# The second MLP product of a decoder step: loads of the squares in GpSimd's queue, other group sizes, kept weights in the last group, and the last norms on VectorE

## The chip, the cores and the metric

The kernel runs as one program on one core of a Trainium2 chip. The metric is the device time of that program in microseconds. Three runs of the kernel before gave 2498.2, 2504.89 and 2498.74 us; their median is 2498.74 us.

## What is computed

One layer of a hybrid decoder for 1024 prompt tokens and 8 x 8 sample tokens (NT = 1088 columns), all in float32. Four token mixers feed a gated output projection; an MLP and a last norm follow. The changed part is the MLP's second product and the last norm:

```python
h2 = rmsnorm(x, p["norm_mlp_g"][l]) * (1.0 + sc2) + sh2
x = x + g2 * (jnp.square(jax.nn.relu(h2 @ p["w_mlp1"][l])) @ p["w_mlp2"][l])
...
y = rmsnorm(x, p["norm_final_g"])        # x * rsqrt(mean(x * x) + 1e-6) * g, over 1024 features
```

`w_mlp1` is 1024 x 4096 and `w_mlp2` 4096 x 1024. In the sample columns the factor g2 differs from sequence to sequence, in the prompt columns it is one number per feature.

## The kernel before, in words

Features lie on partitions in blocks of 128 and tokens in columns. Each float32 operand is split into two parts: `hi`, which ScalarE writes by a copy to the fast matmul type (line 98), and `lo`, the rest, which VectorE gets by a subtraction (line 101). A product is three matmuls, hi by hi, lo by hi and hi by lo (lines 201 to 203). `weights` (lines 151 to 161) loads a weight block of up to 4 x 128 x 128 on SyncE's queue into a tile `wst` (3 buffers) and splits it into `whi` and `wlo` (4 buffers each).

The first MLP product stores its squares in DRAM, as `asc[0]` (hi) and `asc[1]` (lo), 32 blocks k of 128 x 1088 each, by DMAs that GpSimd issues (line 1372). The second product (from line 1389) has 8 output blocks `mt` and 32 blocks k. The k are taken in groups. For each group the kernel loads the group's `ah` and `al` tiles (9 buffers each, 544 KB a tile, line 1422), and for each `mt` it multiplies them with that group's weights in four quarters of 272 columns (two tiles of PSUM with two quarters each, of four such tiles in all) and adds the result, scaled by g2, into the running sum `R[mt]` (`add_resid`). A matmul has 272 columns; one k in one quarter of one `mt` is three of them. The groups are (0,1), (2 to 7), (8 to 15), (16 to 23), (24 to 27) and (28 to 31). The first reads tiles that were kept on the chip (`KK`). A group whose k lie in two weight blocks takes two `wst` for each `mt`, the part with the lower k first. In group 1 the residual `xr` is loaded again and added to each `R[mt]` (lines 1441 to 1444).

The last group is walked in three column ranges: quarters (0,1), quarter 2, quarter 3. Each range goes over all 8 `mt`, with its weights loaded and split anew, and adds the squares of the finished `R[mt]` into `accs` (ScalarE squares into `sqt`, VectorE adds). Behind each range stands its norm (lines 1448 to 1462): a float32 matmul with ones sums `accs` over the partitions (`rms`), ScalarE makes `rstd` by a logarithm and an exponential, and the 8 blocks are scaled and stored as `y`. In the ranges (0,1) and 2, ScalarE multiplies by the gain and GpSimd by `rstd`; in the last range VectorE does both for 6 of 8 blocks.

A scheduler that simulates the program decides the order of each engine's instructions; code under `high_priority` (weights and evacuations, offset 3000) moves ahead of the rest. On the chip each engine runs its list strictly in that order, and an instruction that waits holds all behind it. The DMAs of one engine stand in its list too.

Of the kernel before, what the change touches and what calls it, by code (L numbers as in the profile page):

```python
# [9 lines left out]
F32 = mybir.dt.float32  # L10
# [4 lines left out]
OP = mybir.AluOpType  # L15
# [16 lines left out]
GN_EPS = 64e-5  # L32
LN_EPS = 1e-5
# [57 lines left out]
class Net:  # L91
# [59 lines left out]
    def weights(self, ap, prio=True):  # L151

        with self.tc.high_priority(offset=PRIO) if prio else nullcontext():
            st = self.wp.tile([128, 4, 128], F32, name="wst", tag="wst", bufs=WST)
            hi = self.wp.tile([128, 4, 128], F32R, name="whi", tag="whi", bufs=WHI)
            lo = self.wp.tile([128, 4, 128], F32R, name="wlo", tag="wlo", bufs=WHI)
# [29 lines left out]
    def gemm_quarters(self, parts, X, evac, groups):  # L186
# [4 lines left out]
        for j, (ap, ks) in enumerate(parts):  # L191
            hi, lo = self.weights(ap)
# [894 lines left out]
PRIO = 3000  # L1087
WST, WHI = 3, 4
# [7 lines left out]
def trunk_kernel(ctx: ExitStack, tc: tile.TileContext, A):  # L1096
# [252 lines left out]
    with tc.tile_pool(name="pq", bufs=4, space=PSUM, reuse_waits="tile") as net.pq:  # L1349
# [41 lines left out]
        with ExitStack() as m:  # L1391
# [4 lines left out]
            GROUPS = ((0, 1), (2, 3, 4, 5, 6, 7), tuple(range(8, 16)), tuple(range(16, 24)), (24, 25, 26, 27), (28, 29, 30, 31))  # L1396
# [16 lines left out]
            for gi, ks in enumerate(GROUPS):  # L1413
                final = gi == len(GROUPS) - 1
                Xs = {}
                for k in ks:
                    if gi == 0:
                        Xs[k] = Kept(2 * k), Kept(4 + 2 * k)
                    else:
                        t = [ap_.tile([128, NT], F32R, name=f"a{p}", tag=f"a{p}", bufs=NA) for p in "hl"]  # L1420
                        for x, d in zip(t, asc):
                            nc.sync.dma_start(x.bitcast(F32), d[k].bitcast(F32))
# [14 lines left out]
                for cs in (((0, 1),), ((2,),), ((3,),)) if final else (((0, 1), (2, 3)),):  # L1437
                    for mt in range(8):
                        net.gemm_quarters(parts(ks, mt), Y, ev, cs)
# [5 lines left out]
                    if not final:  # L1445
                        continue

                    ps = net.pqt("rms")
                    for i, q in enumerate(cs[0]):
                        sl = slice(q * QU, q * QU + QU)  # L1450
                        net.mm(ps[:, i, :QU], net.ones, accs[:, sl])
                        net.lnp(rstd[:, sl], ps[:, i, :QU], 1.0 / D, net.eps)
                        net.exph(rstd[:, sl])
                    sl = slice(cs[0][0] * QU, cs[0][-1] * QU + QU)
                    for k in range(KB8):
                        r, t = R[k][:, sl], rstd[:, sl]
                        if cs[0] != (3,) or k % 3 == 2:
                            net.act(r, r, AF.Copy, scale=net.p("norm_final_g", k))
                            nc.gpsimd.tensor_tensor(r, r, t, op=OP.mult)
                        else:  # L1460
                            net.stt(r, r, net.p("norm_final_g", k), t, OP.mult, OP.mult)
                        (nc.sync if k % 2 else nc.scalar).dma_start(A["y"][k][:, sl], r)
# [93 lines left out]
```

## Time and profile before

| | |
|---|---|
| median of three runs | 2498.74 us |
| the profiled execution | 2501.3 us, its span 2499.5 us |
| TensorE matmul | 2419.5 us busy, 97% of the span |
| VectorE, ScalarE, GpSimd | 1383.3 us (55%), 1037.4 us (42%), 331.7 us (13%) |
| mean granted TensorE clock | 0.986 of full speed |
| last column range (0,1) ends | 2449.6 us |

The span runs from the first to the last instruction; the profiled execution is 1.8 us longer than its span. All times below are microseconds from the span's start. "PE" is TensorE's matmul, "PEld" its weight load, which overlaps it, DVE is VectorE, ACT ScalarE, POOL GpSimd, and SPq is SyncE's list of DMA issues. A row that ends in [1.21 <-ACT whi] says that the engine stood idle for 1.21 us before it and which instruction ended that. The clock is given as a share of full speed: 1.00 is 2.4 GHz and 0.50 is 1.2 GHz.

### The profile page before, as it was taken

The numbers are of one execution on the slowest core, as the hardware profiler recorded it, in microseconds if no ns is written. First come the engines' busy times: TensorE is split into PE (matmuls) and PEld (weight loads), VectorE is DVE, ScalarE is ACT, GpSimd is POOL, SyncE is SP. The second block draws the span as 40 slices with busy tenths as digits, with TensorE's granted clock in tenths as the row PEclk, the third lists the DMA queues.
The fourth block names the chain that finished last, engine by engine and source line by source line (L and its number), as shares of the span: only waits on it lengthen the run. The fifth ranks groups of instructions, "written<-read, shape, count | busy, mean of one in ns | idle before, by whom it ended". The sixth has DMA issues, their size and how long they took to land.

```text
span 2499.5 us, 46627 instructions
## 1 busy us (share of the span) xinstructions
PE 2419.5 (97%) x19086; PEld 2248.1 (90%) x19086; DVE 1383.3 (55%) x2536; ACT 1037.4 (42%) x1855; POOL 331.7 (13%) x503
## 2 busy tenths in 40 slices
PE   6999999999999999999999999997999999999996
PEld 2898898998988988889888899997999999999996
DVE  6665626647265573556643767768655552422247
ACT  4513544333354224542346553455666664111115
POOL 3111210103100021010111000000222221000003
PEclk9999999999999999999999999998999999999998
DMA  6323221232321233212322464532655558435244
GB/s 245 121 89 90 67 101 63 78 99 71 105 66 62 83 94 101 73 63 84 97 85 103 143 217 154 177 124 90 174 156 153 154 148 265 148 124 186 63 157 135
DMA packets 185302, 300.46 MB, mean 120 GB/s; under 512 B 57576, under 2 KB 97464, under 8 KB 185088
## 3 DMA queue, kind: packets, MB, share of 16 engines
q1 hardware_dynamic: 134672, 217.79, 27.4%
q0 software_dynamic: 47104, 74.44, 9.8%
q10 hardware_dynamic: 3312, 5.25, 0.6%
q8 instruction: 150, 2.46, 0.4%
q14 instruction: 64, 0.52, 0.1%
HBM read 211.29 MB, written 81.66 MB: 117 GB/s over the span
## 4 chain that ended last, share of the span: by engine, by line
PE 85%; DVE 6%; DMA 3%; ACT 2%; issue 2%; SPq 0%; DVEq 0%; ACTq 0%; POOL 0%; POOLq 0%
PE pg L107 58%; PE pa L107 6%; PE pe L107 4%; PE sm L107 3%; PE pc L107 2%; PE pb L107 2%; PE ada L107 2%; PE pu L107 2%; PE G L107 1%; PE pyr L107 1%; PE po L107 1%; DVE X L101 1%; DMA adaw<-ada 1%; DMA wst<-w 1%; DVE wlo L101 1%
## 5 line engine op out<-in xcount | busy, mean ns | idle before, releaser
L107 PE MATMUL pg<-Hh,whi 128*128 128x362 f32 (+1 forms) x1872 | 627.9, 336 | 6.2 <-ACT Hh L98 4.2
L107 PE MATMUL pg<-Hh,wlo 128*128 128x362 f32 (+1 forms) x1872 | 629.4, 336 | 0.0
L107 PE MATMUL pg<-Hl,whi 128*128 128x362 f32 (+1 forms) x1872 | 620.9, 334 | 0.7 <-DVE Hl L104 0.6
L98 ACT ACTIVATE whi<-wst 128x512 fp32r<-128x512 f32 (+1 forms) x404 | 249.9, 620 | 625.7 <-PE pg L107 546.2
L101 DVE TENSOR_TENSOR wlo<-wst,whi 128x512 fp32r<-128x512 f32 (+1 forms) x404 | 279.9, 694 | 360.4 <-ACT whi L98 359.3
L107 PEld LDWEIGHTS pg<-Hh,whi 128*128 128x128 f32 x1872 | 354.2, 189 | 19.4 <-ACT Hh L98 6.0
L107 PEld LDWEIGHTS pg<-Hh,wlo 128*128 128x128 f32 x1872 | 354.6, 189 | 11.9 <-issue 4.2
L107 PEld LDWEIGHTS pg<-Hl,whi 128*128 128x128 f32 x1872 | 353.5, 189 | 10.1 <-issue 2.5
L107 PE MATMUL pg<-ah,whi 128*128 128x272 f32 x960 | 277.1, 291 | 3.7 <-ACT whi L98 3.7
L107 PE MATMUL pg<-ah,wlo 128*128 128x272 f32 x960 | 278.0, 291 | 1.1 <-DVE wlo L101 1.1
L107 PE MATMUL pg<-al,whi 128*128 128x272 f32 x960 | 274.4, 290 | 0.0
L107 PEld LDWEIGHTS pg<-ah,whi 128*128 128x128 f32 x960 | 182.5, 191 | 4.3 <-ACT whi L98 4.2
L107 PEld LDWEIGHTS pg<-ah,wlo 128*128 128x128 f32 x960 | 182.6, 190 | 1.9 <-DVE wlo L101 1.8
L107 PEld LDWEIGHTS pg<-al,whi 128*128 128x128 f32 x960 | 181.0, 190 | 0.0
L104 DVE SCALAR_TENSOR_TENSOR cacc<-u,pv,cacc 128x1024 f32<-128x1024 f32 x120 | 153.7, 1281 | 2.1
L104 DVE SCALAR_TENSOR_TENSOR R<-pg,mod,R 128x544 f32<-128x544 f32 (+2 forms) x120 | 65.7, 570 | 138.0 <-PE pg L107 138.0
L107 PE MATMUL pg<-yh,whi 128*128 128x362 f32 (+1 forms) x384 | 128.3, 334 | 1.2 <-DVE gt L101 1.1
L107 PE MATMUL pg<-yh,wlo 128*128 128x362 f32 (+1 forms) x384 | 127.2, 331 | 0.0
L107 PE MATMUL pg<-yl,whi 128*128 128x362 f32 (+1 forms) x384 | 126.8, 330 | 0.0
L1181 POOL DMA_DIRECT2D g<-gst x96 | 53.5, 557 | 385.2 <-ACT gst L98 370.3
L98 ACT ACTIVATE gst<-pg 128x362 f32<-128x362 f32 (+1 forms) x96 | 45.5, 473 | 130.5 <-PE pg L107 118.9
L693 POOL TENSOR_SCALAR sp<-St,dec 128x64 f32<-128x64 f32 x60 | 56.5, 942 | 222.8 <-DVE St L104 201.3
(446 smaller groups left out, 4818.3 us busy)
## 6 DMA issues: line engine op xcount, KB each, us to landing
wst<-w SPq DMA_DIRECT2D x136, 256.0 KB, 2.9
wst<-w_in SPq DMA_DIRECT2D x92, 256.0 KB, 2.8
gt<-g SPq DMA_DIRECT2D x32, 544.0 KB, 3.8
wst<-w_gate SPq DMA_DIRECT2D x64, 256.0 KB, 3.1
adaw<-ada SPq DMA_DIRECT2D x32, 512.0 KB, 5.3
ah<-ah POOLq DMA_DIRECT2D x60, 272.0 KB, 2.6
al<-al POOLq DMA_DIRECT2D x60, 272.0 KB, 4.3
ah<-ah SPq DMA_DIRECT2D x30, 544.0 KB, 9.6
```

Source lines behind the costliest of these rows:

```text
L98: return self.nc.scalar.activation(out, in_, func, bias=bias, scale=scale)
L101: return self.nc.vector.tensor_tensor(out, a, b, op=op)
L104: return self.nc.vector.scalar_tensor_tensor(out, a, s, b, op0=op0, op1=op1)
L107: return self.nc.tensor.matmul(out, lhsT, rhs, start=start, stop=stop, skip_group_check=True)
L693: nc.gpsimd.tensor_scalar(sp, St, dec[:, c:c + 1], None, op0=OP.mult)
L1181: nc.gpsimd.dma_start(d[:, n0:n0 + n], t[:, :n])
```

## The change

The loads of `ah` and `al` move from SyncE's list to GpSimd's. The groups become (0,1), (2,3), (4 to 11), (12 to 19), (20 to 27) and (28 to 31). `weights` can take another pool: the last group splits its 8 weight blocks once, into 8 buffers each that lie in memory that `KK` had, and all three column ranges use them. The norm of a range is written behind the third `mt` of the next range, and it is done by VectorE alone; only in the last range 2 of 8 blocks still go by ScalarE and GpSimd, as before. Two constants move to the head of the file.

```diff
-    def weights(self, ap, prio=True):
+    def weights(self, ap, prio=True, pool=None, bufs=WHI):
...
-            hi = self.wp.tile([128, 4, 128], F32R, name="whi", tag="whi", bufs=WHI)
-            lo = self.wp.tile([128, 4, 128], F32R, name="wlo", tag="wlo", bufs=WHI)
+            hi = (pool or self.wp).tile([128, 4, 128], F32R, name="whi", tag="whi", bufs=bufs)
+            lo = (pool or self.wp).tile([128, 4, 128], F32R, name="wlo", tag="wlo", bufs=bufs)
...
-        for j, (ap, ks) in enumerate(parts):
-            hi, lo = self.weights(ap)
+        for j, (W, ks) in enumerate(parts):
+            hi, lo = W if isinstance(W, tuple) else self.weights(W)
...
-            GROUPS = ((0, 1), (2, 3, 4, 5, 6, 7), tuple(range(8, 16)), tuple(range(16, 24)), (24, 25, 26, 27), (28, 29, 30, 31))
+            GROUPS = ((0, 1), (2, 3)) + tuple(tuple(range(i, i + 8)) for i in (4, 12, 20)) + ((28, 29, 30, 31),)
...
-                            nc.sync.dma_start(x.bitcast(F32), d[k].bitcast(F32))
+                            nc.gpsimd.dma_start(x.bitcast(F32), d[k].bitcast(F32))
...
-                for cs in (((0, 1),), ((2,),), ((3,),)) if final else (((0, 1), (2, 3)),):
+                def last_norm(qs):
+                    sl = slice(qs[0] * QU, qs[-1] * QU + QU)
+                    ps = net.pqt("rms")
+                    for i, q in enumerate(qs):
+                        s = slice(q * QU, q * QU + QU)
+                        net.mm(ps[:, i, :QU], net.ones, accs[:, s])
+                        net.lnp(rstd[:, s], ps[:, i, :QU], 1.0 / D, net.eps)
+                        net.exph(rstd[:, s])
+                    for k in range(KB8):
+                        r, t = R[k][:, sl], rstd[:, sl]
+                        if qs == (3,) and k % 3 == 2:
+                            net.act(r, r, AF.Copy, scale=net.p("norm_final_g", k))
+                            nc.gpsimd.tensor_tensor(r, r, t, op=OP.mult)
+                        else:
+                            net.stt(r, r, net.p("norm_final_g", k), t, OP.mult, OP.mult)
+                        (nc.sync if k % 2 else nc.scalar).dma_start(A["y"][k][:, sl], r)
+
+                columns = ((0, 1), (2,), (3,)) if final else (((0, 1), (2, 3)),)
+                if final:
+                    last.close()
+                    fw, kept = right(m, "fw"), []
+                for n, qs in enumerate(columns):
                     for mt in range(8):
-                        net.gemm_quarters(parts(ks, mt), Y, ev, cs)
+                        if not final:
+                            net.gemm_quarters(parts(ks, mt), Y, ev, qs)
+                        else:
+                            if n == 0:
+                                kept.append(net.weights(A["w2"][ks[0] // 4, mt], pool=fw, bufs=8))
+                            net.gemm_quarters([(kept[mt], ks)], Y, ev, (qs,))
...
-                    ps = net.pqt("rms")
...
-                        if cs[0] != (3,) or k % 3 == 2:
...
+                        if final and n and mt == 2:
+                            last_norm(columns[n - 1])
+                if final:
+                    last_norm(columns[-1])
```

SyncE's list where the second product begins, before; `wst` are weights (256 columns: two k, 512: four k), `xr` the residual:

```order
L159 DMA wst<-w 128x256
L1422 DMA ah<-ah 128x1088
L1422 DMA al<-al 128x1088
L1443 DMA xr<-xsp 128x544 x2
L1422 DMA ah<-ah 128x1088
L159 DMA wst<-w 128x512
L1422 DMA al<-al 128x1088
L1422 DMA ah<-ah 128x1088
```

The same place now, from the weights of group 0 on:

```order
L161 DMA wst<-w 128x256 x8
L1469 DMA xr<-xsp 128x544 x2
L161 DMA wst<-w 128x256 x7
L1469 DMA xr<-xsp 128x544 x2
L161 DMA wst<-w 128x256
L161 DMA wst<-w 128x512 x2
L1469 DMA xr<-xsp 128x544 x2
L161 DMA wst<-w 128x512 x3
```

The loads of `ah` and `al` have left the list; the weights of group 1 now stand right behind the first `xr`, and each later `xr` stands between weights.

VectorE's list in group 1, before: the evacuation of one `mt` (R_21773 is the second), the split of later weights, and the residual:

```order
L104 SCALAR_TENSOR_TENSOR R_21773<-pg,mod,R_21773 128x544
L104 SCALAR_TENSOR_TENSOR R_21773<-pg,mod,R_21773 128x272
L104 SCALAR_TENSOR_TENSOR R_21773<-pg,mod,R_21773 128x208
L101 TENSOR_TENSOR t_22279<-pg,mod 128x64
L101 TENSOR_TENSOR wlo<-wst,whi 128x512
L101 TENSOR_TENSOR R_21773<-R_21773,t_22279 128x64
L101 TENSOR_TENSOR R_21773<-R_21773,xr 128x1088
L101 TENSOR_TENSOR wlo<-wst,whi 128x256
```

Now, at the sixth `mt` of group 1 (R_21777); the first `wlo` belongs to the seventh `mt`, the second to the eighth:

```order
L106 SCALAR_TENSOR_TENSOR R_21777<-pg,mod,R_21777 128x544
L106 SCALAR_TENSOR_TENSOR R_21777<-pg,mod,R_21777 128x272
L106 SCALAR_TENSOR_TENSOR R_21777<-pg,mod,R_21777 128x208
L103 TENSOR_TENSOR t_22323<-pg,mod 128x64
L103 TENSOR_TENSOR R_21777<-R_21777,t_22323 128x64
L103 TENSOR_TENSOR wlo<-wst,whi 128x256
L103 TENSOR_TENSOR R_21773<-R_21773,xr 128x1088
L106 SCALAR_TENSOR_TENSOR R_21778<-pg,mod,R_21778 128x544
L103 TENSOR_TENSOR wlo<-wst,whi 128x256
```

The seventh block's `wlo` now stands behind the whole evacuation of the sixth, and R_21773's residual is added only there.

VectorE's list in the last group, before: the end of the range of quarter 2:

```order
L101 TENSOR_TENSOR wlo<-wst,whi 128x512
L104 SCALAR_TENSOR_TENSOR R_21776<-pg,mod,R_21776 128x272
L101 TENSOR_TENSOR accs<-accs,sqt 128x272
L101 TENSOR_TENSOR wlo<-wst,whi 128x512
L104 SCALAR_TENSOR_TENSOR R_21777<-pg,mod,R_21777 128x272
L101 TENSOR_TENSOR accs<-accs,sqt 128x272
L101 TENSOR_TENSOR wlo<-wst,whi 128x512
L104 SCALAR_TENSOR_TENSOR R_21778<-pg,mod,R_21778 128x272
```

Now, the same range (R_21777 with 272 columns from PSUM is its sixth `mt`):

```order
L103 TENSOR_TENSOR accs<-accs,sqt 128x272
L106 SCALAR_TENSOR_TENSOR R_21772<-R_21772,pv,rstd_21781 128x544
L106 SCALAR_TENSOR_TENSOR R_21773<-R_21773,pv,rstd_21781 128x544
L106 SCALAR_TENSOR_TENSOR R_21777<-pg,mod,R_21777 128x272
L106 SCALAR_TENSOR_TENSOR R_21774<-R_21774,pv,rstd_21781 128x544
L106 SCALAR_TENSOR_TENSOR R_21775<-R_21775,pv,rstd_21781 128x544
L106 SCALAR_TENSOR_TENSOR R_21776<-R_21776,pv,rstd_21781 128x544
L106 SCALAR_TENSOR_TENSOR R_21777<-R_21777,pv,rstd_21781 128x544
L106 SCALAR_TENSOR_TENSOR R_21778<-R_21778,pv,rstd_21781 128x544
L106 SCALAR_TENSOR_TENSOR R_21779<-R_21779,pv,rstd_21781 128x544
L106 SCALAR_TENSOR_TENSOR R_21778<-pg,mod,R_21778 128x272
L103 TENSOR_TENSOR accs<-accs,sqt 128x272
```

No `wlo` is left there; eight scalings of 544 columns by `rstd` stand among the evacuations, six of them in a row ahead of that of the seventh `mt`.

## Rows read from the trace of the kernel before

**Rows 1.** The first part of the page: busy us of each engine, share of the span, instructions.

```profile
PE 2419.5 (97%) x19086; PEld 2248.1 (90%) x19086; DVE 1383.3 (55%) x2536; ACT 1037.4 (42%) x1855; POOL 331.7 (13%) x503
```

**Rows 2.** The view of stretches: us, then each engine's busy us (and instructions), the granted clock, the DMA engines' mean share and GB/s.

```profile
2100.00:2150.00 50.00, 45.11 (x331) 44.07 (x330) 17.85 (x37) 8.41 (x17) 0.00 (x0) 0.93 0.58 202
2250.00:2300.00 50.00, 50.00 (x401) 50.00 (x400) 11.05 (x24) 5.06 (x8) 0.00 (x0) 1.00 0.59 220
```

**Rows 3.** TensorE's timeline, the rows with idle time ahead of them from 2103 us on: start, duration, instruction, count, and in brackets the idle time and what ended it.

```profile
2104.49 0.52 PE L107 MATMUL pg<-ah,whi 128*128 128x272 f32 x2 [1.21 <-ACT whi L98]
2110.51 0.82 PE L107 MATMUL pg<-ah,whi 128*128 128x272 f32 x2 [2.54 <-ACT whi L98]
2121.15 0.39 PE L107 MATMUL pg<-ah,wlo 128*128 128x272 f32 x1 [1.15 <-DVE wlo L101]
2451.99 0.70 PE L107 MATMUL rms<-accs,ones 128*128 128x272 f32 x2 [2.41 <-DVE accs L101]
2473.52 1.28 PE L107 MATMUL rms<-accs,ones 128*128 128x272 f32 x2 [8.22 <-DVE accs L101]
2490.97 0.70 PE L107 MATMUL rms<-accs,ones 128*128 128x272 f32 x2 [2.52 <-DVE accs L101]
```

**Rows 4.** The chain that ended last, in order of time (start, us, what): three of its pieces.

```profile
2121.15 328.44 PE pg L107 x2614
2449.61 0.80 DVE R L104
...
2494.70 1.65 DVE R L104 x4
```

**Rows 5.** The view of stretches in steps of 5 us, columns as in rows 2.

```profile
2105.00:2110.00 5.00, 2.97 (x23) 2.75 (x22) 0.00 (x0) 0.17 (x1) 0.00 (x0) 1.00 1.04 420
2110.00:2115.00 5.00, 4.49 (x18) 4.26 (x19) 0.69 (x1) 0.46 (x1) 0.00 (x0) 0.50 1.02 405
2115.00:2120.00 5.00, 5.00 (x34) 4.78 (x32) 0.99 (x2) 1.47 (x3) 0.00 (x0) 0.82 0.29 101
...
2450.00:2455.00 5.00, 3.01 (x22) 2.96 (x23) 2.31 (x5) 3.32 (x7) 0.00 (x0) 1.00 0.22 59
...
2470.00:2475.00 5.00, 1.48 (x4) 1.25 (x5) 3.47 (x7) 2.58 (x6) 0.86 (x1) 0.50 0.76 226
```

**Rows 6.** SyncE's list on the timeline, weights (line 159), and below them GpSimd's first store after 2070 us.

```profile
2059.92 21.00 SPq L159 DMA_DIRECT2D wst<-w  x6
2088.61 0.33 SPq L159 DMA_DIRECT2D wst<-w  x1
2100.26 0.33 SPq L159 DMA_DIRECT2D wst<-w  x1
2081.49 0.67 POOL L1372 DMA_DIRECT2D ah<-ah  x1 [12.01 <-ACT ah L98]
```

**Rows 7.** The DMA view: issues, KB each, median us to landing. The first two rows are of 2084 to 2103 us, the last of 1990 to 2075 us.

```profile
al<-al POOLq DMA_DIRECT2D x3, 272.0 KB, 12.3
wst<-w SPq DMA_DIRECT2D x1, 128.0 KB, 14.1
wst<-w SPq DMA_DIRECT2D x7, 128.0 KB, 2.6
```

**Rows 8.** GpSimd's DMA issues in the whole span (count, busy us, mean ns of one), and the landing times of its 16 stores of mixer outputs, 544 KB each.

```profile
L1372 POOL DMA_DIRECT2D al<-al x68 | 49.7, 814 | 44.4 <-DVE al L101 37.3 <-DVE R L101 4.2 <-DVE wlo L101 2.8
L1084 POOL DMA_DIRECT2D y<-lig x4 | 2.2, 542 | 4.0 <-DVE St L104 3.2 <-DVE lig L101 0.7
DMA to landing us min/median/max: 2.9/4.1/8.5
```

**Rows 9.** The first load for group 3 in SyncE's list, and the landing times of the 21 loads of `ah` from 2160 to 2400 us.

```profile
2273.43 0.33 SPq L1422 DMA_DIRECT2D ah<-ah  x1
DMA to landing us min/median/max: 8.5/9.5/10.6
```

**Rows 10.** The last evacuation of group 0 on ScalarE (it waits for the end of the matmuls), and the split on VectorE that ends TensorE's wait at 2121.15.

```profile
2103.32 0.81 ACT L98 ACTIVATE R<-pg,mod 128x272 f32<-128x272 f32 x2 [0.78 <-PE pg L107]
2120.68 0.41 DVE L101 TENSOR_TENSOR wlo<-wst,whi 128x256 fp32r<-128x256 f32 x1
```

**Rows 11.** VectorE's groups by shape, mean ns of one and idle time ahead: the first three from 2410 us on, the last three from 2150 to 2410 us.

```profile
L101 DVE TENSOR_TENSOR wlo<-wst,whi 128x512 fp32r<-128x512 f32 x23 | 20.7, 901 | 0.7 <-ACT whi L98 0.7
L101 DVE TENSOR_TENSOR accs<-accs,sqt 128x272 f32<-128x272 f32 x14 | 9.7, 691 | 0.6 <-ACT sqt L98 0.5
L101 DVE TENSOR_TENSOR accs<-accs,sqt 128x544 f32<-128x544 f32 x7 | 5.1, 726 | 0.9
L101 DVE TENSOR_TENSOR wlo<-wst,whi 128x512 fp32r<-128x512 f32 x43 | 29.5, 686 | 83.7 <-ACT whi L98 83.7
L104 DVE SCALAR_TENSOR_TENSOR R<-pg,mod,R 128x544 f32<-128x544 f32 x25 | 19.6, 784 | 44.0 <-PE pg L107 44.0
L101 DVE TENSOR_TENSOR R<-R,xr 128x1088 f32<-128x1088 f32 x5 | 6.5, 1292 | 0.3 <-DMA xr<-xsp 0.2
```

**Rows 12.** GpSimd's timeline in the last group: the multiplications by `rstd` of the range (0,1).

```profile
2457.97 12.88 POOL L1459 TENSOR_TENSOR R<-R,rstd 128x544 f32<-128x544 f32 x8 [363.25 <-ACT rstd L98]
```

**Rows 13.** ScalarE's timeline at the end: the logarithm behind the last `rms`, and the exponential.

```profile
2491.70 0.49 ACT L98 ACTIVATE rstd<-rms,epst 128x272 f32<-128x272 f32 x1 [1.35 <-PE rms L107]
2492.22 0.43 ACT L98 ACTIVATE rstd<-rstd 128x272 f32<-128x272 f32 x1
```

More of the change, by code (lines that the diff above doesn't have):

```diff
@@ L32 @@
 GN_EPS = 64e-5
+PRIO = 3000
+WST, WHI = 3, 4
 LN_EPS = 1e-5
@@ L1084, in lru_block @@
         nc.gpsimd.dma_start(self.ysc[3][j], hs[:, :NT])
-PRIO = 3000
-WST, WHI = 3, 4
 NG = 5
@@ L1444, in trunk_kernel @@
                             net.tt(R[mt], R[mt], x, OP.add)
-                    if not final:
-                        continue
-                    ps = net.pqt("rms")
[L1449 to L1456, printed above, removed]
-                        if cs[0] != (3,) or k % 3 == 2:
[L1458 to L1462, printed above, removed]
-    last.close()
+                        if final and n and mt == 2:
+                            last_norm(columns[n - 1])
+                if final:
+                    last_norm(columns[-1])
 def _pack(i):
```

## The prediction

> **What bounds the kernel now.** TensorE is busy for 97% of the span [rows 1], so first its pace, then its gaps. In the chain that ended last, one piece of 2614 matmuls in 328.44 us [rows 4] gives 0.12565 us a matmul; across group changes it has no gap (50.00 of 50.00 us busy and clock 1.00 [rows 2]). So the product can gain only at its two ends.
>
> At the beginning TensorE ends group 0 at 2103.28 (its next row starts at 2104.49 after 1.21 us idle [rows 3]; ScalarE's evacuation starts at 2103.32 [rows 10]). It waits 1.21, 2.54 and 1.15 us, and after the second wait the clock is 0.50 for 5 us and 0.82 for the next 5 [rows 3, 5]. From 2103.28 to 2121.15 it does 74 matmuls (2688 from the start of group 1 to the end of the range (0,1), less the 2614). At pace they take 9.3 us, so 8.6 of the 17.87 us are lost. The cause stands in SyncE's list: a block of weights is issued only at 2100.26, behind thirteen loads of squares [rows 6], while the DMA engines are full (share 1.04, 420 GB/s [rows 5]).
>
> At the end the range (0,1) is over at 2449.6 [rows 4] and the last `rms` starts at 2490.97 [rows 3]: 41.4 us for 192 matmuls (24.1 us) and three `rms` of 0.70 us (2.1). About 15 us are lost: TensorE waits 2.41, 8.22 and 2.52 us for `accs` [rows 3], and with the second wait the clock is at 0.50 again [rows 5]. VectorE is late because GpSimd multiplies beside it, 8 times 1.6 us [rows 12]: a split of weights takes 901 ns there against 686 in the middle, and an addition of 272 columns nearly as long as one of 544 (691 to 726) [rows 11].
>
> **The change, part by part.** The sum is made against the profiled execution (span 2499.5 us, 1.8 us around it). That execution is 2.6 us above the median of the runs, so the difference is taken off the median.
>
> *Loads and groups at the beginning.* The weights of group 1 stand right behind group 0's. Split number 9 (its first `mt`) can be issued when group 0's sixth block is split, about 2087 (before, it stood behind ten loads and went at 2088.61 [rows 6]). Group 1 needs it at 2103.3. Landing is between 2.6 us and 14.1 us (the same 128 KB in an idle stretch, and behind the squares [rows 7]); even the upper end gives 2101, 2102 with its split, and the next blocks come every 3 us, as their need does. So the waits of 1.21 and 2.54 us go, and the slow clock with them. The squares cannot start earlier: GpSimd's first load stands behind its store of 2081.49 [rows 6], as SyncE's did behind its weights until 2080.92. The four tiles for group 1 have 20 us; even the 14.1 us would do. The other fourteen early tiles, 7.6 MB at some 400 GB/s, are in by about 2110; group 2 begins at 2128. If the cover by distance failed, the cost is the old 8.6 us.
>
> *A new wait in group 1.* The seventh block's `wlo` stands on VectorE behind the whole evacuation of the sixth, and that needs TensorE's last matmul of the sixth. This is the wait of 1.15 us at 2121.15 once more (there too the split follows the evacuation), with one addition of 64 columns more. It waits for no DMA, only for its place. I take 1.2 us; bounds 0.9 (pipelined closer) and 1.6. Behind it stand the residual of the second block and the last two evacuations; TensorE has two PSUM tiles free then, so nothing else is late. All other `wlo` of group 1 stand ahead of their need.
>
> So the range (0,1) ends at 2103.28 + 2688 x 0.12565 + 1.2 = 2442.2 instead of 2449.6: minus 7.4 us.
>
> *Loads from GpSimd in the middle.* 60 loads of 544 KB move to GpSimd's list. Its stores of that size take 542 ns to issue, its stores of half the size 814 on the mean in bursts beside VectorE's work [rows 8]. Nothing else stands in its list there but the last stores of squares. The critical loads are those of the second k of a group: SyncE issued its like at 2273.43 [rows 9], 7.3 us ahead of the group's first matmul (group 3 starts at 2280.7 by the pace), and it came in time. In GpSimd's queue a 544 KB transfer landed in 2.9 to 8.5 us [rows 8], in SyncE's bursts in 8.5 to 10.6 [rows 9]. At 2.9 plus two issues it is there 3 us early. At 8.5 it is 1 to 2 us late, at four places (three changes, and k = 11 in group 2, which has 8 us): plus 6 us. I take 0, because the slower landings of SyncE's queue cost nothing, and keep 6.
>
> At one place a rule of the Trainium skill speaks against this part. The page "SBUF — State Buffer", in "A bandwidth-pool intuition that's wrong (but worth ruling out)", says that a DMA from GpSimd's queue can take about 3100 ns instead of 620 beside a VectorE copy, because GpSimd cannot write descriptors while VectorE holds the port that both share. Its section "Who interferes with whom" adds that an operation on two tensors takes only the reading side, which would spare these loads. The trace bears the second out so far: its issues stay at 542 to 814 ns on the mean beside such work. By the first the sum would be that of rival 1, and with the page's 3.1 us an issue an estimated 2539 us.
>
> *The last group.* Its 192 + 192 matmuls are the same. 16 of 24 splits go from ScalarE and VectorE, and GpSimd's share of the first two norms goes with its slowing. VectorE gets eight scalings of 544 columns (bounds 726 and 784 ns, the addition and the evacuation of that width [rows 11]; I take 0.74) and eight of 272 (0.41, from four in 1.65 us [rows 4]).
>
> I follow the lists from T, the end of the range (0,1). TensorE: three blocks, `rms` of quarter 0 at T+4.5 (its `accs` is ready at T+2.9, so that wait is gone), two blocks, `rms` of quarter 1 until T+9.1. ScalarE has `rstd` at T+10.4 (logarithm 0.49, a square 0.43, exponential 0.43 [rows 13]). VectorE then does two scalings, one evacuation, six scalings, and reaches the seventh block's evacuation at T+16.9, though TensorE was done with it at T+12.0. TensorE has four PSUM tiles; its third block of quarter 3 needs that one, at T+16.5, and gets it at T+17.25: 0.75 us idle. The `rms` of quarter 2, due at T+18.8, waits for the `accs` behind the next evacuations until T+20.2: 1.4 us. Five blocks more end at T+28.4. The scalings of quarter 2 keep VectorE until T+26, so the last evacuations and sums end at T+32.1, 3.7 us behind TensorE (it was 2.9). From there all is as before: 2490.97 to 2499.5, 8.5 us. So 32.1 us stand where 41.4 stood: minus 9.3 us.
>
> The clock should hold: an idle time of 2.41 us at 2450 left it at 1.00 [rows 5], 3.75 us within 7 at 2104 to 2110 did not; 2.15 us within 4 lies between.
>
> **Sum.** -7.4 - 9.3 = -16.7 us: 2498.74 - 16.7 = 2482.0. Without the two waits in the last group and the one in group 1 it would be 3.4 us less, 2478.7.
>
> **The rivals.**
>
> 1. *Slower than before: GpSimd's issues are held up by VectorE.* If an issue takes x us, a group of 8 has 14 loads to make between 7.3 us ahead of its start and the need of its last k, which in group 3 before came 132 matmuls or 16.6 us after it: 24 us, less some 4 for the landing. They are late from x = 1.4 on. Two such changes, and the last group's 6 loads in 12 us less 4, cost 2(14x - 20) + (6x - 8); this eats the 16.7 us at x = 1.9. An issue of 0.81 us that first waits out VectorE's longest operation here (1.29 us, the addition of the residual [rows 11]) takes 2.1 us: 23 us late, 2505. Against it: issues beside VectorE's work stay at 0.81 us [rows 8]. For it: no load of this shape in that queue in the trace, and GpSimd's multiplications beside VectorE did slow each other [rows 11, 12]. Chance 0.06.
>
> 2. *The beginning stays.* The DMA engines are full from 2084 to 2115 whoever issues, and GpSimd's stores of 272 KB landed in 12.3 us beside SyncE's squares [rows 7]: a queue of its own does not make a transfer quick. Then the 7.4 us stay: 2489.4. Against it: 14.1 us still suffice. Chance 0.11.
>
> 3. *VectorE's backlog lets the clock fall.* If after the two waits near T+17 to T+20 the clock is 0.50 for 5 us and 0.82 for 5, as after 2110 [rows 5], 3.4 us are lost: 2485.4. Chance 0.13.
>
> 4. *Late landings at the group changes,* as bounded above: 2488. Chance 0.10.
>
> 5. *The edit does not do what it says:* a wait that I missed keeps both ends, within 0.3% of before. Chance 0.05.
>
> **How the numbers follow.** Forecast 0.55 (2478 to 2485). The range from 2477 to 2493 takes in rivals 2 to 4 and leaves out 1, 5 and the joint cases of 2 with 4. 0.3% is 7.5 us, about what a measurement of this kernel can tell from no change; faster by more means below 2491.2: the forecast, rivals 3 and 4 and a third of rival 2, 0.82; within 0.3%: rival 5, the rest of rival 2 (its joint cases with 3 or 4) and the milder part of rival 1, 0.13; slower: rival 1 with longer issues, 0.05.
>
> **What would show it.** In the new profile: no idle row of TensorE between 2103 and 2108; one of about 1.2 us near 2121 released by `wlo`; the last `mt` of the range (0,1) evacuated near 2442; GpSimd's load issues under 1 us and no wait of TensorE on a DMA at the group changes; VectorE's additions of 272 columns well below their 0.69 us; two idle rows of about 1 us near T+17 and T+19, clock 1.00; the last `rms` at T+32. I am wrong if weights still land behind squares, if a group change has a gap, or if a wait longer than 3 us stands in the last group.

## The result and the profile after

The changed kernel takes 2487.02 us (median of 4 runs, 2486.74 to 2488.59) where the kernel before took 2498.76 beside it (2498.2 to 2504.89): 11.7 us less by the medians. The ratio of the two kernels is put at 0.9944, 95% interval 0.9931 to 0.9956, or 11.0 to 17.2 us. The forecast of 2482.0 was 5 us too low. The time lies in its range of 2477 to 2493, though outside the 2478 to 2485 to which it gave a chance of 0.55. Between the two profiled executions the span went from 2499.5 to 2485.1 us, 14.4 us. TensorE's busy time answers to [rows 1]:

```profile
PE 2410.5 (97%) x19086; PEld 2236.8 (90%) x19086; DVE 1373.5 (55%) x2536; ACT 1018.2 (41%) x1823; POOL 343.4 (14%) x547
```

Four places of the trace divide the 14.4 us: the end of group 0, the end T of the column range (0,1) (VectorE starts its last evacuation of 544 columns there), the first matmul of the last `rms`, and the end of the span.

| stretch | before | after | difference | forecast |
|---|---|---|---|---|
| start to end of group 0 | 2103.28 | 2102.50 | -0.8 | 0 |
| group 0 to T | 346.3 | 340.9 | -5.4 | -7.4 |
| T to last `rms` | 41.4 | 30.9 | -10.5 | -9.3 |
| last `rms` to end of span | 8.5 | 10.8 | +2.2 | 0 |

TensorE's timeline of the changed kernel, all its rows with idle time between 2103 us and the end, answers to [rows 3] (start, duration, instruction, idle time and what ended it):

```profile
2122.32 0.40 PE L109 MATMUL pg<-ah,wlo 128*128 128x272 f32 x1 [1.42 <-DVE wlo L103]
2340.03 0.39 PE L109 MATMUL pg<-al,whi 128*128 128x272 f32 x1 [0.31 <-DMA al<-al]
2459.79 0.39 PE L109 MATMUL pg<-ah,whi 128*128 128x272 f32 x1 [0.37 <-DVE R L106]
2462.54 0.73 PE L109 MATMUL rms<-accs,ones 128*128 128x272 f32 x2 [1.00 <-DVE accs L103]
2474.33 1.00 PE L109 MATMUL rms<-accs,ones 128*128 128x272 f32 x2 [3.65 <-DVE accs L103]
```

Where 3.75 us of idle time stood in two waits on `whi` at the beginning, none is left. The wait on `wlo` near 2122 is the one that the forecast added (1.2 us; it took 1.42), and the two before T+20 are its two waits of the last group (T is 2443.43; 0.75 and 1.4 were forecast, 0.37 and 1.00 came). The row of 0.31 us released by a transfer of `al` stands at a group change; the forecast took nothing there. The view of stretches shows the clock, as [rows 5] did:

```profile
2105.00:2110.00 5.00, 5.00 (x42) 5.00 (x41) 4.24 (x11) 0.84 (x2) 2.28 (x4) 1.00 1.19 395
2110.00:2115.00 5.00, 5.00 (x42) 5.00 (x41) 3.84 (x11) 0.34 (x1) 0.00 (x0) 1.00 1.03 389
2120.00:2125.00 5.00, 3.58 (x29) 3.37 (x28) 3.71 (x8) 0.71 (x2) 0.00 (x0) 1.00 0.25 65
2460.00:2465.00 5.00, 4.00 (x30) 3.71 (x30) 4.59 (x17) 3.00 (x8) 0.00 (x0) 1.00 0.28 99
```

The clock is 1.00 where it was 0.50 at 2110, and it stays there through the two waits near T+20 of the last group. The DMA engines are as full as before (1.19 and 1.03). What changed at the beginning stands in SyncE's list, where the first row follows the weights of group 0 without a load of squares between, and on GpSimd, whose loads are shown by the view of one line (answers to [rows 6, 8, 9]):

```profile
2086.30 21.06 SPq L161 DMA_DIRECT2D wst<-w  x7
L1422 POOL DMA_DIRECT2D ah<-ah x30: 531/531/734, 2082.8 to 2414.3; - x30
L1422 POOL DMA_DIRECT2D al<-al x30: 531/531/731, 2083.3 to 2414.8; - x30
DMA to landing us min/median/max: 4.0/10.4/13.2
```

An issue takes 531 ns (minimum, median) to 734 at the most: VectorE does not hold GpSimd up. In the last group VectorE's additions of 272 columns take 438 ns where they took 691 [rows 11], from 2410 us on:

```profile
L103 DVE TENSOR_TENSOR accs<-accs,sqt 128x272 f32<-128x272 f32 x14 | 6.1, 438 | 3.3 <-ACT sqt L100 3.0
L106 DVE SCALAR_TENSOR_TENSOR R<-R,pv,rstd 128x544 f32<-128x544 f32 x8 | 5.7, 776 | 0.0
```

What the forecast did not have is the end of the program. In steps of 1 us, the first two rows of the kernel before and then two of the changed one (last columns: granted clock, DMA share, GB/s):

```profile
2497.00:2498.00 1.00, 0.00 (x0) 0.00 (x0) 0.00 (x0) 0.00 (x0) 0.00 (x0) 0.50 1.04 361
2498.00:2499.00 1.00, 0.00 (x0) 0.00 (x0) 0.00 (x0) 0.00 (x0) 0.00 (x0) 0.50 0.03 10
```
```profile
2481.00:2482.00 1.00, 0.00 (x0) 0.00 (x0) 0.00 (x0) 0.00 (x0) 0.00 (x0) 0.50 0.61 212
2482.00:2483.00 1.00, 0.00 (x0) 0.00 (x0) 0.00 (x0) 0.00 (x0) 0.00 (x0) 0.50 0.00 0
```

The transfers end near 2498.1 and 2481.6, the spans at 2499.5 and 2485.1: after the last byte pass 1.4 us before and 3.5 after.

### The profile page after: what moved, and what is told of

It is laid out like the page before. It is cut to its first block, busy times and chain, and to the rows that moved or that the text cites. A ratio compares the mean times of both kernels' runs of the same rounds, so it can differ in the third digit from the quotient of the medians.

```text
span 2485.1 us, 46469 instructions
## 1 busy us (share of the span) xinstructions
PE 2410.5 (97%) x19086; PEld 2236.8 (90%) x19086; DVE 1373.5 (55%) x2536; ACT 1018.2 (41%) x1823; POOL 343.4 (14%) x547
## 4 chain that ended last, share of the span: by engine, by line
PE 76%; issue 10%; DVE 6%; DMA 5%; ACT 2%; POOL 0%; ACTq 0%; DVEq 0%; POOLq 0%
PE pg L109 49%; PE pa L109 6%; PE pe L109 4%; PE sm L109 3%; PE pc L109 2%; PE ada L109 2%; PE pb L109 2%; PE pu L109 2%; DMA ah<-ah 1%; PE G L109 1%; PE pyr L109 1%; PE po L109 1%; DMA al<-al 1%; DMA adaw<-ada 1%; DVE X L103 1%
## 5 line engine op out<-in xcount | busy, mean ns | idle before, releaser
L100 ACT ACTIVATE whi<-wst 128x512 fp32r<-128x512 f32 (+1 forms) x388 | 239.9, 620 | 582.3 <-PE pg L109 504.0
L103 DVE TENSOR_TENSOR wlo<-wst,whi 128x512 fp32r<-128x512 f32 (+1 forms) x388 | 264.1, 682 | 367.9 <-ACT whi L100 366.4
```

The costliest lines, as they stand in the source:

```text
L100: return self.nc.scalar.activation(out, in_, func, bias=bias, scale=scale)
L103: return self.nc.vector.tensor_tensor(out, a, b, op=op)
```

## The experiments

Twelve runs were made, in four sets, each set on a chip of its own and beside the kernel before on that chip. The table gives the three stretches of each profiled execution (group 0 to T, T to the last `rms`, from there to the end), the median and the difference of the median to the kernel before beside it.

| kernel | group 0 to T | to last `rms` | to the end | median | difference |
|---|---|---|---|---|---|
| before_again | 343.5 | 42.7 | 8.5 | 2499.81 | +0.8 |
| after_again | 341.1 | 30.9 | 11.1 | 2486.98 | -14.0 |
| loads_on_sync | 348.8 | 30.9 | 9.0 | 2494.63 | -4.4 |
| old_groups | 338.7 | 30.9 | 10.9 | 2483.52 | -15.5 |
| wlo_gpsimd | 339.4 | 30.9 | 10.7 | 2483.78 | -15.1 |
| last_loads_sync | 344.7 | 30.9 | 10.4 | 2489.27 | -9.6 |
| old_end | 341.2 | 44.6 | 10.7 | 2498.57 | -0.5 |
| split_again | 340.3 | 34.1 | 10.5 | 2490.30 | -10.7 |
| gpsimd_norms | 341.0 | 29.5 | 10.8 | 2485.30 | -15.7 |
| norm_at_once | 340.5 | 37.2 | 10.5 | 2491.24 | -9.7 |
| best | 338.0 | 31.5 | 9.4 | 2482.25 | -16.6 |
| parts_together | 338.0 | 29.4 | 9.0 | 2480.60 | -19.6 |

A median moves by what happens ahead of the product too: group 0 ended between 2098.5 and 2105.3 us in these executions, with the code ahead of it unchanged. So the stretches decide, though each comes from a single profiled execution.

**before_again** and **after_again**: no edit.

> The kernel before, unchanged, profiled a second time. The first profiled execution was 2501.3 us, 2.6 above the median of its runs, and the forecast was set against it. Theory A (the 2.6 us belong to that one execution): this profile has a span near 2497; the matmuls from the start of group 1 to the end of the range (0,1) take 346.3 us again, the last group 41.4, and the difference lies ahead of group 1 or behind the last rms. Theory B (the beginning of the product differs from run to run): the stretch from group 1's start to the end of the range (0,1) is about 2.6 us shorter than 346.3, and the changed kernel gained less there than its profile says.

> The changed kernel, unchanged, profiled a second time beside its variants, since the start of group 1 lay between 2099.3 and 2105.7 us in the profiles so far and the median on one chip need not be that on another. Theory A (its stretches repeat): 340.9 us from the start of group 1 to the end of the range (0,1), 30.9 us from there to the last rms, 10.4 us from there to the end of the span; the ratio to before is 0.9944 within its interval. Rival B (the profile of it was a lucky one): one of the three stretches is over 1 us longer.

The second profile of before has much the same waits at the beginning, but there the clock holds (second wait, and the view of stretches). In the last group it is the other way round: behind the first wait the clock falls (last two rows):

```profile
2111.32 0.52 PE L107 MATMUL pg<-ah,whi 128*128 128x272 f32 x2 [2.16 <-ACT whi L98]
2110.00:2115.00 5.00, 3.47 (x25) 3.25 (x26) 0.69 (x1) 0.63 (x1) 0.00 (x0) 1.00 1.03 414
2450.32 0.70 PE L107 MATMUL rms<-accs,ones 128*128 128x272 f32 x2 [2.42 <-DVE accs L101]
2450.00:2455.00 5.00, 4.68 (x23) 4.64 (x24) 1.36 (x3) 2.60 (x6) 0.00 (x0) 0.66 0.20 56
```

Theory B is right: the stretch is 2.8 us shorter (343.5 for 346.3), for a clock of 1.00 where it was 0.50 in [rows 5], behind waits of 1.21 and 2.16 us instead of 1.21 and 2.54. So the beginning gave 5.4 us against the one profile and 2.4 against the other. The last group is 1.3 us longer than in the first profile (42.7 for 41.4): the clock is 0.66 on the mean from 2450 to 2455, part of that time at its lower level of 0.50, where [rows 5] had 1.00. The changed kernel's stretches repeat within 0.3 us (theory A), its median beside before was 14.0 us lower, ratio 0.995 (0.9937 to 0.9962).

**loads_on_sync**:

```diff
-                            nc.gpsimd.dma_start(x.bitcast(F32), d[k].bitcast(F32))
+                            nc.sync.dma_start(x.bitcast(F32), d[k].bitcast(F32))
```

> The changed kernel with the loads of squares back in SyncE's list; groups, kept weights and norms stay changed. In that list the first weights of group 1 stand behind eight loads and the second behind thirteen. Theory A (the place behind the loads makes the weights late): the waits of TensorE on whi near 2104 and 2110 and the clock of 0.50 are back, the stretch from group 1's start to the end of the range (0,1) is 343 to 346 us instead of 340.9, and the time is 2489 to 2492. Rival B (the small second group does it, since its four tiles leave the DMA engines early): no such wait, 341 us, within 1 us of 2487.0. In the middle A and B both expect the two short waits at the group changes (0.3 us each) to go or to stay, 0.5 us at most.

```profile
2107.78 0.82 PE L109 MATMUL pg<-ah,whi 128*128 128x272 f32 x2 [3.73 <-ACT whi L100]
2115.01 0.85 PE L109 MATMUL pg<-ah,whi 128*128 128x272 f32 x4 [1.41 <-ACT whi L100]
2105.00:2110.00 5.00, 2.22 (x10) 2.22 (x11) 2.00 (x4) 0.42 (x1) 0.00 (x0) 0.70 1.04 412
```

Theory A, and more than it expected: the two waits on `whi` are 3.73 and 1.41 us, the clock falls to 0.70, and the stretch is 348.8 us, longer than in the kernel before. The second block of weights stands behind thirteen loads, as in the kernel before, and is late again. In the groups of before that block holds four k and feeds TensorE for 6 us; here it holds two, 3 us, and the third block is late too. So the small second group without the queue makes the beginning worse. The end of the span is short again, 9.0 us.

**old_groups**:

```diff
-            GROUPS = ((0, 1), (2, 3)) + tuple(tuple(range(i, i + 8)) for i in (4, 12, 20)) + ((28, 29, 30, 31),)
+            GROUPS = ((0, 1), (2, 3, 4, 5, 6, 7), tuple(range(8, 16)), tuple(range(16, 24)), (24, 25, 26, 27), (28, 29, 30, 31))
```

> The changed kernel with the groups of before (2, 6, 8, 8, 4, 4); the loads stay in GpSimd's list. Theory A (the queue is what counts): the weights of group 1 no longer stand behind squares, there is no wait on whi longer than 1 us near 2103 to 2111, and the clock stays at 1.00; the time is within 1.5 us of 2487.0. Rival B (the groups count): the block of six k brings two pieces of weights for each mt through a DMA that is full from 2084 to 2115 us, TensorE waits 2 to 5 us and the clock falls; 2491 to 2495.

Theory A: no idle row at the beginning at all.

```profile
2100.00:2105.00 5.00, 5.00 (x42) 5.00 (x42) 1.34 (x3) 1.28 (x4) 1.59 (x3) 1.00 1.16 390
2120.00:2125.00 5.00, 5.00 (x42) 5.00 (x41) 2.07 (x3) 0.42 (x1) 0.00 (x0) 1.00 0.57 193
2273.97 0.39 PE L109 MATMUL pg<-al,whi 128*128 128x272 f32 x1 [0.17 <-DMA al<-al]
```

TensorE is busy in all of 2100 to 2125, with the DMA engines at a share of 1.16. The stretch is 338.7 us against 337.7 for 2688 matmuls at the pace of [rows 4], 0.12565 us each: the new groups cost the changed kernel 2.3 us, most of it the wait on `wlo`, which does not appear with six k in the group.

**wlo_gpsimd**, which moves the one `wlo` on which TensorE waits:

```diff
+                        if gi == 1 and mt == 6:
...
+                                net.act(W[0], st)
+                                nc.gpsimd.tensor_tensor(W[1], st, W[0].bitcast(F32), op=OP.subtract)
```

> The changed kernel with one subtraction moved: the wlo of the seventh block of group 1, on which TensorE waits 1.4 us near 2122, is made by GpSimd instead of VectorE, where it stands behind the evacuation of the sixth block. Theory A (its place in VectorE's list is the wait): its weights land and whi is ready about 1.3 us ahead of TensorE's need, GpSimd needs about 0.8 us for 256 columns, and the wait goes; 339.4 to 339.8 us from the start of group 1 to the end of the range (0,1) instead of 340.9 to 341.1. Rival B (its weights are late, because the DMA is full until 2115): the wait stays at 1 us or more.

GpSimd's row:

```profile
2112.18 0.73 POOL L1466 TENSOR_TENSOR wlo<-wst,whi 128x256 fp32r<-128x256 f32 x1 [5.27 <-ACT whi L100]
```

Theory A: it is done at 2112.9, and TensorE's idle row is gone (339.4 us; what is left near 2121 is 0.33 us above pace). The weights had been there; only the place in VectorE's list was late.

**last_loads_sync**:

```diff
-                            nc.gpsimd.dma_start(x.bitcast(F32), d[k].bitcast(F32))
+                            (nc.gpsimd if gi < 5 else nc.sync).dma_start(x.bitcast(F32), d[k].bitcast(F32))
```

> The changed kernel with the loads of the last group alone (8 of 60) back in SyncE's list. In all profiles with the loads in GpSimd's list the span ends 3.1 to 3.5 us after the last DMA activity, in the others 1.2 to 1.5 us; from the last rms to the end that is 10.4 to 11.1 us against 8.5 to 9.0. Theory A (the end of the program takes longer with the number of loads that GpSimd has issued): 52 of 60 remain, so 10.2 to 10.8 us. Rival B (it takes longer because GpSimd's loads stand near the end): 8.5 to 9.0 us, and the time is 2 us below the changed kernel. The rest is as in the changed kernel.

The end takes 10.4 us: not rival B, and the number fits theory A. The lines of the queues (packets, MB, share) put the kernels in order, first the kernel before, then best (28 loads by GpSimd), last_loads_sync (52) and the changed kernel (60):

```profile
q0 software_dynamic: 47104, 74.44, 9.8%
```
```profile
q0 software_dynamic: 51136, 90.04, 11.5%
```
```profile
q0 software_dynamic: 54592, 103.41, 12.9%
```
```profile
q0 software_dynamic: 55744, 107.87, 13.4%
```

From the last transfer of `y` to the end of the span they have 1.4, 1.6, 2.9 and 3.5 us. That more loads in GpSimd's queue go with a longer end is shown, but not in proportion: the first 28 add 0.2 us, the other 32 add 1.9. Whether their number counts or how late in the program they stand is open, and which instruction takes the time no profile shows. This execution also had the latest landings at the change to the group (20 to 27):

```profile
2328.12 0.39 PE L109 MATMUL pg<-al,whi 128*128 128x272 f32 x1 [1.45 <-DMA al<-al]
2340.27 0.40 PE L109 MATMUL pg<-ah,whi 128*128 128x272 f32 x1 [0.86 <-DMA ah<-ah]
2320.99 0.33 SPq L1422 DMA_DIRECT2D ah<-ah  x1
2328.60 0.53 POOL L1422 DMA_DIRECT2D al<-al  x1 [2.18 <-DMA al<-al]
```

All its waits on transfers sum to 3.7 us (0.52, 0.28, 0.28, 1.45, 0.86, 0.32), those of after_again to 0.7 (0.18, 0.22, 0.34): most of the 3.6 us between their first stretches. Most of it is the edit's own doing: SyncE issues the first load of the last group at 2320.99 (the third row) and its `al` at 2321.50, while GpSimd still has four loads of the group (20 to 27) to issue, until 2328.60 (the fourth row). In the changed kernel these two loads of 544 KB are the last of the sixteen in GpSimd's list (2329.86 and 2331.32). The DMA engines are full from 2320 to 2340 in both (shares of 1.01 to 1.03), so two transfers that are not yet needed go ahead of some that are. The median agrees: it is 9.6 us below before, those of the changed kernel 11.7 and 14.0.

**old_end**: the last group's code of before on the changed kernel (splits for every range, ScalarE and GpSimd in the first two norms, each norm behind its range).

> The changed kernel with the last group of before: weights split again for each range of columns, first two norms with ScalarE and GpSimd, each norm written right behind its range. The beginning and the middle stay changed. Theory A (the two ends are independent): the beginning gives its 5.4 us by the two profiles, the last group takes 41.4 us from the end of the range (0,1) to the last rms again, and the time is 2492 to 2494. Rival B (the forecast's size of the beginning, 7.4 us, is right and the profile of before was off): 2491.3. Rival C (the changed kernel's beginning gives nothing by itself): 2498.

The time is that of rival C (-0.5 us), but not for its reason, and A and B are out. The beginning is the changed one (341.2), but the last group took 44.6 us, 1.9 to 3.2 more than in the two profiles of before, and the end 2.2 more; together they eat the beginning's gain. Some 1.5 of the 3.2 us against the first profile come behind the first wait, where the clock falls as in before_again (the row stands in the last section). The rest comes in the last range, where ScalarE waits 3.81 us for a block of weights and VectorE then 2.00 us for its `whi`; in the kernel before it was 1.98 and 0.17. Why that block landed later is open.

```profile
2479.44 0.63 ACT L100 ACTIVATE whi<-wst 128x512 fp32r<-128x512 f32 x1 [3.81 <-DMA wst<-w]
2480.10 0.69 DVE L103 TENSOR_TENSOR wlo<-wst,whi 128x512 fp32r<-128x512 f32 x1 [2.00 <-ACT whi L100]
```

VectorE's rows also show which of its operations suffer beside GpSimd's multiplications:

```profile
2453.63 1.58 DVE L103 TENSOR_TENSOR accs<-accs,sqt 128x272 f32<-128x272 f32 x1
2455.14 0.49 DVE L106 SCALAR_TENSOR_TENSOR R<-pg,mod,R 128x272 f32<-128x272 f32 x1
```

The addition of 272 columns that reads two tensors in SBUF takes 1.58 us, the evacuation of the same width, which reads PSUM and one tensor, 0.49 as ever.

**split_again**, **gpsimd_norms** and **norm_at_once** each undo one part of the last group:

```diff
-                            if n == 0:
-                                kept.append(net.weights(A["w2"][ks[0] // 4, mt], pool=fw, bufs=8))
-                            net.gemm_quarters([(kept[mt], ks)], Y, ev, (qs,))
+                            net.gemm_quarters(parts(ks, mt), Y, ev, (qs,))
```

```diff
-                        if qs == (3,) and k % 3 == 2:
+                        if qs != (3,) or k % 3 == 2:
```

```diff
-                        if final and n and mt == 2:
-                            last_norm(columns[n - 1])
-                if final:
-                    last_norm(columns[-1])
+                    if final:
+                        last_norm(qs)
```

> The changed kernel, but the last group's weights are loaded and split again for each range of columns; norms as changed. Theory A (kept weights matter through VectorE, which bounds the last group): 16 splits of 0.69 us come back to VectorE, 11 us; it has 2.2 us idle in the last group, so the last rms comes 7 to 10 us later than 30.9 us behind the range (0,1), and the time is 7 to 10 us above the changed kernel. Rival B (GpSimd's slowing was the whole loss, so the splits fit between the matmuls): 30.9 to 33 us, at most 2 us above.

> The changed kernel, but the first two norms are done by ScalarE and GpSimd as before (still written behind the third mt of the next range, weights kept). Theory A (GpSimd's 16 multiplications slow VectorE, but they also take 9.3 us of scalings off it): VectorE's additions of 272 columns take over 0.7 us beside them instead of 0.43, its scalar_tensor_tensor operations stay at 0.49; last rms 30 to 33 us behind the range (0,1), within 2 us of the changed kernel. Rival B (GpSimd was the cause of the last group's loss): 36 to 41 us, 5 to 10 us above. Rival C (VectorE's scalings are the new bound, and moving them off it helps): 27 to 29 us, 2 to 4 us below.

> The changed kernel, but each norm is written right behind its range of columns instead of behind the third mt of the next. Theory A (the place matters because TensorE stands still for accs): TensorE waits 2.4 us for accs behind the range (0,1) again and 1.5 to 3 us behind quarter 2, the clock may fall after it; 33 to 37 us from the range (0,1) to the last rms, 2 to 6 us above the changed kernel. Rival B (the earlier norm gives VectorE its scalings earlier, when it has idle time, and makes up for the wait): 30 to 32 us, no difference.

```profile
2458.49 0.39 PE L109 MATMUL pg<-ah,wlo 128*128 128x272 f32 x1 [1.92 <-DVE wlo L103]
2471.50 0.37 PE L109 MATMUL pg<-ah,whi 128*128 128x272 f32 x1 [1.99 <-DVE t L103]
```
```profile
2453.95 18.07 POOL L1449 TENSOR_TENSOR R<-R,rstd 128x544 f32<-128x544 f32 x16 [37.92 <-ACT rstd L100]
2473.54 1.24 PE L109 MATMUL rms<-accs,ones 128*128 128x272 f32 x2 [4.11 <-DVE accs L103]
```
```profile
2448.55 0.70 PE L109 MATMUL rms<-accs,ones 128*128 128x272 f32 x2 [2.75 <-DVE accs L103]
2466.65 1.19 PE L109 MATMUL rms<-accs,ones 128*128 128x272 f32 x2 [2.19 <-DVE accs L103]
2482.99 0.70 PE L109 MATMUL rms<-accs,ones 128*128 128x272 f32 x2 [2.17 <-DVE accs L103]
2450.00:2455.00 5.00, 5.00 (x29) 4.92 (x29) 1.18 (x3) 1.30 (x4) 0.00 (x0) 0.69 0.02 3
```

Splitting again costs 3.2 us (34.1), between theory A's 7 to 10 and rival B's 2: TensorE waits 1.92 us for a `wlo` and 1.99 behind an evacuation, but most of the 11 us of splits find idle time. The norm written at once costs 6.3 us in the profile (37.2) and 4.3 by the medians, theory A: three waits for `accs` of 2.17 to 2.75 us, and the clock at 0.69 behind the first (this profile was the slowest of its five runs). With GpSimd back in the norms the last group is 1.5 us *shorter* (29.5), between theory A and rival C; rival B is out. Its 16 multiplications take 18 us, but VectorE has no scalings and TensorE waits nowhere except for the last `accs`.

**best** and **parts_together** put together what the runs favoured:

```diff
-            GROUPS = ((0, 1), (2, 3)) + tuple(tuple(range(i, i + 8)) for i in (4, 12, 20)) + ((28, 29, 30, 31),)
+            GROUPS = ((0, 1), (2, 3, 4, 5, 6, 7), tuple(range(8, 16)), tuple(range(16, 24)), (24, 25, 26, 27), (28, 29, 30, 31))
...
-                            nc.gpsimd.dma_start(x.bitcast(F32), d[k].bitcast(F32))
+                            (nc.gpsimd if gi < 3 else nc.sync).dma_start(x.bitcast(F32), d[k].bitcast(F32))
...
-                        if qs == (3,) and k % 3 == 2:
+                        if (qs == (3,) and k % 3 == 2) or (qs == (0, 1) and k % 2):
```

The last line is that of best; parts_together has `if qs != (3,) or k % 3 == 2:` there.

> What the runs so far favour, together: the groups of before (2, 6, 8, 8, 4, 4); the loads of squares of the second and third group in GpSimd's list (28 of 56), the later ones in SyncE's; kept weights and late norms as changed, but of the norm of the range (0,1) every second multiplication by ScalarE and GpSimd. Theory A (each part adds up): 338.5 us from the start of group 1 to the end of the range (0,1) (no wait on wlo), 29 to 30.5 us to the last rms, 9 to 10 us from there (28 loads instead of 60 by GpSimd, if the longer end goes by their number), 4 us below the changed kernel: 2481 to 2484. Rival B (GpSimd's multiplications slow VectorE's additions as much as they relieve it): 31 to 32 us in the last group, 2484 to 2486. Rival C (loads in SyncE's list hold weights up in the middle too): a wait on whi over 1 us at a group change after 2230.

> The kernel called best, but with the first two norms wholly by ScalarE and GpSimd (late, weights kept), since in best a scaling of 544 columns on VectorE took 1786 ns beside GpSimd's multiplications and 779 without them, while the run with all 16 multiplications on GpSimd had 29.45 us in the last group. Theory A (two engines that both read two tensors in SBUF slow each other, so the work should go to one of them): 338.0 us from the start of group 1 to the end of the range (0,1), 29.4 us to the last rms, 9.4 us to the end; 2 us below best by these stretches, 2479 to 2482. Rival B (GpSimd alone is no better when the quarter-2 norm comes 1 us earlier or later against the additions of 64 columns, which took 676 ns beside it instead of 220): 31 us or more in the last group, no difference to best.

VectorE's group of scalings in best, and the page's first part for parts_together:

```profile
L106 DVE SCALAR_TENSOR_TENSOR R<-R,pv,rstd 128x544 f32<-128x544 f32 x4 | 7.0, 1786 | 0.0
```
```profile
PE 2407.7 (97%) x19086; PEld 2235.2 (90%) x19086; DVE 1369.6 (55%) x2520; ACT 1028.4 (42%) x1839; POOL 344.0 (14%) x531
```

In best the beginning and the end came as theory A said (338.0 and 9.4), the last group as rival B said (31.5), and the wait of rival C did not come: a scaling on VectorE beside GpSimd's multiplications takes 1786 ns instead of 776, so the halves cost more than either whole. With all of it on GpSimd the three stretches are 338.0, 29.4 and 9.0 us, as expected, and the median is 2480.60 us: ratio to before 0.992 (0.9906 to 0.9933), where after_again had 0.995. It has the lowest median of all, and its interval lies below that of after_again (the two ran on different chips, each beside the kernel before).

## Why the prediction was right, and where its terms were off

The mechanism was right at the beginning and in the main in the last group, and the terms were off. Of the 5 us that the forecast was too low, 2.3 stand in the terms (14.4 us between the profiles for 16.7). The rest is its starting point: it took a difference against a profiled execution that it knew to be 2.6 us above the median off that median, and that execution was one with a slow clock at the beginning. That 2487 lies near the numbers of rivals 3 and 4 (2485.4 and 2488) is chance, since neither happened at its size.

*Weights behind squares at the beginning:* right. loads_on_sync brings the waits and the slow clock back, and old_groups shows that the queue alone does it. Oversized: the 8.6 us lost were those of one execution, whose clock fell; the other profile of before lost 2.8 us less. Rival 2 (a queue of its own does not make a transfer quick) is out: TensorE had no wait on `whi` with the DMA engines full.

*The new wait in group 1:* right in place and cause (wlo_gpsimd), 1.42 us for 1.2. The forecast did not see that it is the price of the group (2, 3), which brought nothing: the groups of before have no wait there.

*Loads in the middle at nothing:* mis-sized, not wrong. Landings of 4.0 to 13.2 us cost 0.3 and 0.7 us in the two profiles of the changed kernel, which is rival 4 at a twentieth to an eighth of its 6 us. The margin is thin: two loads issued ahead of their turn in last_loads_sync brought 2.6 us of waits at one change (3.7 in all).

*Issues held up by VectorE (rival 1):* out, 531 to 734 ns for all 60. So is rival 5: both ends changed as described. Of the two rules of the Trainium skill ("SBUF — State Buffer") that the forecast set against each other, the one in "Who interferes with whom", that VectorE's operations on two tensors spare such loads, agrees with these rows; the stall of "A bandwidth-pool intuition that's wrong (but worth ruling out)" beside a copy no run here shows. The 3.1 us that the forecast put on one issue are in that section the time of a whole transfer.

*The last group:* -9.3 forecast, -10.5 to -11.8 measured, and its two waits stand where they were put. The clock held through them, so rival 3 is out. But the step that named the cause failed in part: "VectorE is late because GpSimd multiplies beside it". The slowing is real (1.58 us for an addition), yet with weights kept and norms late GpSimd's norms are the faster choice by 1.5 us. What paid is the later place (6.3 us by the profile of norm_at_once, 4.3 by its median) and the kept weights (3.2 by split_again); the part "without GpSimd" lost. One by one these make 8.0 us (6.3 + 3.2 - 1.5), less than the 10.5 that the change brought, so the parts act on each other. What GpSimd cost in the old last group, with its splits and early norms, no run took out alone. How VectorE and GpSimd share is told by the Trainium skill, "SBUF — State Buffer", section "Who interferes with whom": a VectorE instruction with two inputs in SBUF contends with GpSimd instructions that read SBUF, one with at most one such input, outside the two-port modes, does not. The rows agree: 1.58 and 1786 ns on the one side, 0.49 us on the other.

*"From there all is as before: 8.5 us":* this step failed, by 2.2 to 2.5 us. The forecast had no term there. The end of the program grew with the loads in GpSimd's queue: 3.5 us pass behind the last transfer where 1.4 did, and 1.4 again in loads_on_sync, which has the changed last group without those loads.

So of the -16.7 us, 2.2 to 2.5 went into the end, 2.0 (or 5.0 by the second profile of before) were missing at the beginning, and 1.2 to 2.5 came in addition in the last group.

## What to carry to other kernels

Look which list a critical transfer stands in before asking how full the DMA engines are: the same bytes cost nothing once the weights did not stand behind them. Move only the loads that need it: 28 early ones in GpSimd's queue went with 0.2 us more at the program's end, 60 with 2.1. When some loads move to another list, look which of them now go ahead of more urgent ones. Where VectorE and GpSimd can both do a piece of elementwise work on tensors in SBUF, try giving it wholly to the one with idle time, late enough that nobody waits: here a half share was 0.6 to 2.1 us slower than either whole.

## What was not expected of the hardware

The span ends 1.4 us after the last transfer with no squares loaded by GpSimd and 3.5 us after it with 60 loads; with 28 and 52 it is 1.6 and 2.9. A scaling that reads two tensors in SBUF slows from 776 to 1786 ns beside GpSimd's multiplications, an evacuation from PSUM not at all. After waits of the same size the clock fell in one execution and held in another: 0.50 and 1.00 in the two profiles of before at 2110 us, and 0.66 on the mean in old_end from 2445 us on and in before_again from 2450, behind a wait of 2.42 us, where it stayed at 1.00 behind 2.41 us in [rows 3, 5]:

```profile
2444.36 0.70 PE L109 MATMUL rms<-accs,ones 128*128 128x272 f32 x2 [2.42 <-DVE accs L103]
2445.00:2450.00 5.00, 5.00 (x29) 4.95 (x27) 1.55 (x3) 2.77 (x6) 0.00 (x0) 0.66 0.13 45
```
